# Scores of 64-feature heads with both parts of the queries stacked over 128 rows

## The chip, the cores and the metric

The kernel runs on one core of one Trainium2 chip. The metric is the device time of one launch in microseconds, taken as the median over several runs. TensorE does the matmuls (PE in the profile; its loads of the stationary operand are PEld), VectorE is DVE, ScalarE is ACT, GpSimd is POOL, and SyncE (SP) issues most transfers.

## The reference

Two layers of a decoder trunk over 512 tokens of 1024 features, batch 1, all in float32. Of a layer, what matters here is the attention of mixers A and B, whose heads have 64 features:

```python
# A, for each of 3 head groups of 8 heads; the first group has window 128, dilation 1
logits = jnp.einsum('brnqhd,brnkhd->brnhqk', qb, kb).astype(jnp.float32) * (dh ** -0.5)
bias = bias_table[t5_bucket(step * dilation)].astype(jnp.float32).transpose(2, 0, 1)
logits = jnp.where(valid[None, None, :, None], logits + bias, NEG)
# B: 8 query heads on 2 key heads, window 128, banded blocks
logits = jnp.einsum('bnqhgd,bnchd->bnhgqc', qb, kb).astype(jnp.float32) * (dh ** -0.5)
logits = jnp.where(valid[None, :, None, None], logits + bias, NEG)
# softmax and values follow; C is a latent attention; then gates, output projection, a layer norm,
# a gated feed-forward with a causal convolution (w=3), and a second layer norm
```

With blocks of 128 queries, an undilated A head or a B head looks at its own block of 128 keys and the one before it (the first block at its own alone).

## The kernel before

**Numbers in two parts.** Every matmul operand is kept as a high part, rounded to the type fp32r, and a low part, the rest. `split_to` makes them: ScalarE copies the source into the high part (L177, or L180 with a scale) and VectorE subtracts that from the source (L178, or L181). `mm3` (L171 to L173) adds three products, high by high, low by high and high by low. Weights go the same way: a transfer brings 512 KB, ScalarE and VectorE split it (L76, L77), two pieces ahead of their use.

**Jobs and items.** A job holds the queries and keys of two heads, made by one 128-column projection each (`o1`, 24 matmuls of 512 columns into a bank of the tag `mm`, tiles `qkp`), so that head 0 lies on rows 0 to 63 and head 1 on rows 64 to 127. A layer has 12 A jobs, 4 of them undilated (group g = 0), and 4 B jobs, which share one pair of key heads (`project_bkv`). Each job has four items, one for each block of 128 queries. An item's `scores` makes the scores (tiles `scp`) in PSUM banks of the tag `sc`, of which there are two, and VectorE adds the bias and takes the maximum (L486), ScalarE the exponentials (L489); `turn` transposes them (`ptp`, L500) and splits them (`pT`); `values` multiplies by the values (`op`).

**Three forms of scores.** Dilated A jobs (g > 0) are "joint": the keys are laid out block-diagonally, and one `mm3` over all 128 rows makes both heads' scores in one bank. The others take one bank for each head and three matmuls for each head, ordered so that the two heads alternate; in undilated A and B these use 64 rows (head 0 the upper half, head 1 the lower), in C 96 rows:

```python
pp = [s_bank("scp")[:, :n] for _ in range(2)]
ops = [j.qk(h, slice(t * P, (t + 1) * P), slice(k0, k0 + n)) for h in range(2)]
for a, b, first, last in ((0, 2, True, False), (0, 3, False, False), (1, 2, False, True)):
    for p, o in zip(pp, ops):
        nc.tensor.matmul(p, o[a], o[b], start=first, stop=last)
```

Here n is 256 columns, or 128 for the first block.

**What sets the order.** Projections call `gap`, which starts items as a budget of time allows; a scheduler then places every engine's instructions by readiness and priority, so items of A and B come to stand between the matmuls of the projections and gates that follow, and an item's matmuls may stand apart. Each engine runs its own list in order. Tiles of 1024 columns (queries, keys, values, `pT` and others) come from one pool of 22 slots.

Of the kernel before, what the change touches and what calls it, by code (L numbers as in the profile page):

```python
# [133 lines left out]
def hybrid_trunk(ctx: ExitStack, tc: tile.TileContext, I, out):  # L134
# [20 lines left out]
    def s_bank(name):  # L155
        return bank("sc", 2, name)
# [10 lines left out]
    def slot(name, dtype=F32):  # L167
        return sp.tile([P, 1024], dtype, name=name, tag="s")
# [203 lines left out]
    for l in range(DEPTH):  # L372
# [87 lines left out]
        class Item:  # L460
# [6 lines left out]
            def scores(self):  # L467
                j, t = self.job, self.t
                nk = len(j.keys(t))
                n = nk * P  # L470
                self.sb = tp.tile([P, 512], F32, name="sb", tag="sb", bufs=4) if nk <= 2 else slot("sb")
                self.st = j.stats(t, self)
                v = self.sb[:, :2 * n].rearrange("p (h k) -> p h k", h=2)
                k0 = j.keys(t)[0] * P
                if j.joint:
                    p = s_bank("scp")
                    pp = [p[:, h * n:(h + 1) * n] for h in range(2)]
                    mm3(p[:, :2 * n], *j.qk_joint(slice(t * P, (t + 1) * P), slice(k0, k0 + n)), True, True)
                else:
                    pp = [s_bank("scp")[:, :n] for _ in range(2)]  # L480
                    ops = [j.qk(h, slice(t * P, (t + 1) * P), slice(k0, k0 + n)) for h in range(2)]
# [3 lines that stand above are left out]
                for h in range(2):  # L485
                    nc.vector.tensor_tensor_reduce(v[:, h, :], pp[h], j.bias(h, nk), -j.scale, j.floor(h),  # L486
                                                   ALU.add, ALU.min, self.st[:, h:h + 1])
                for h in range(2):
                    nc.scalar.activation(v[:, h, :], v[:, h, :], AF.Exp, bias=self.st[:, h:h + 1], scale=-1.0,  # L489
                                         accum_out=self.st[:, 2 + h:3 + h])  # L490
# [33 lines left out]
                else:  # L524
                    j.finish(t, self, o)

        def halves(h, q, k, qs, ks):
            b = slice(h * 64, h * 64 + 64)
            return q[b, 0, qs], q[b, 1, qs], k[b, 0, ks], k[b, 1, ks]

        def block_diagonal(src):

# [12 lines left out]
        class JobA:  # L545
# [2 lines left out]

            def __init__(self, hf, g, c, bv, vv):
                self.hf, self.g, self.c, self.bv, self.vv = hf, g, c, bv, vv  # L550
                self.joint = g > 0
                self.vt, self.vh = 2, 2 * c

            def normalize(self, item, n):
# [8 lines left out]
            def stats(self, t, item):  # L563
                item.row = tp.tile([P, 132], F32, name="row", tag="row", bufs=4)
                return item.row[:, P:]

            def qk(self, h, qs, ks):
                return halves(h, self.q, self.k, qs, ks)

            def qk_joint(self, qs, ks):  # L570
                return self.q[:, 0, qs], self.q[:, 1, qs], self.k[0][:, :, ks], self.k[1][:, :, ks]
# [51 lines left out]
        def project_a(l, j):  # L623
# [8 lines left out]
            for c in range(2):  # L632
                job = JobA(hf, g, c, bv, vv)
                for nm in ("q", "k"):
                    w = W.next((l, (j, nm, c)), KT, P)
                    p = mm_bank("qkp")
                    o1(p, w, 0, xT, gap)
                    if g and nm == "k":
                        job.k = block_diagonal(p.rearrange("p (i r) -> p r i", r=4))
                        gap(UNIT / 2)  # L640
                        continue
                    r = slot(nm, F32R).rearrange("p (a n) -> p a n", a=2)
                    setattr(job, nm, r)
                    src, dh, dl = p[:, :], r[:, 0, :], r[:, 1, :]
                    if g:
                        src = src.rearrange("p (i r) -> p r i", r=4)
                        dh, dl = (a.rearrange("p (r i) -> p r i", r=4) for a in (dh, dl))
                    split_to(dh, dl, src, 0.125 if nm == "q" else None)
                    gap(UNIT / 2)
                att.queue.extend(Item(job, t) for t in range(NT))  # L650
            if j % 3 == 2:
# [1 line left out]

        class JobB(JobA):

            g, mixer, joint, direct, vt, vh = 0, 1, False, True, NT, 0

            def __init__(self, i):
                self.i = self.c = i
# [20 lines left out]
            def project(self, l, bv, kv):  # L680
                self.bv, (self.k, self.vv) = bv, kv
                p = mm_bank("qkp")
                o1(p, W.next((l, "bq", self.i), KT, P), 0, xT, gap)
                self.q = slot("q", F32R).rearrange("p (a n) -> p a n", a=2)
                split_to(self.q[:, 0, :], self.q[:, 1, :], p[:, :], 0.125)
                gap(UNIT / 2)

        def scale_rows(item, n):
# [6 lines left out]

        def project_bkv(l):
            w = W.next((l, "bk"), KT, P)
            kk = slot("bk", F32R).rearrange("p (a n) -> p a n", a=2)
            vv = slot("bv", F32R).rearrange("p (t h a d) -> p t h a d", t=4, h=2, a=2)
            p = mm_bank("qkp")  # L700
            o1(p, w, 0, xT, gap)
            split_to(kk[:, 0, :], kk[:, 1, :], p[:, :])
            gap(UNIT / 2)
            p = mm_bank("vp")
            o1(p, W.next((l, "bv"), KT, P), 0, xT, gap)
# [9 lines left out]

        class JobC:

            scale, mixer, joint, direct, vt, vh = C_SCALE, 2, False, True, NT, 0

            def __init__(self, c):  # L720
                self.c = c
# [370 lines left out]
```

## Time and profile before

| | |
|---|---|
| median of 3 runs | 2124.74 us (2123.12 to 2124.78) |
| the profiled execution's own time | 2121.85 us |
| its span, from the first to the last instruction | 2120.0 us |
| PE busy | 2084.7 us, 98% |
| DVE busy | 1198.1 us, 57% |
| ACT busy | 889.9 us, 42% |
| mean TensorE clock granted | 0.998 |

The profile is of one execution. A matmul's row gives its start and its length; successive matmuls overlap in the records, so what one costs the stream is the distance from its start to the next start. Names such as `scp<-k,q` say what is written and, behind the arrow, what is read; a form such as `64*128 64x256` says 64 rows by 128 columns of stationary operand, and 256 columns moved.

### The profile page before, as it was taken

How to read it: one execution, taken by the hardware profiler on the slowest of the kernel's cores; microseconds unless marked ns; L12 is line 12 of the kernel's file. 1: busy time of each engine (PE TensorE's matmuls, PEld its weight loads, DVE VectorE, ACT ScalarE, POOL GpSimd, SP SyncE). 2: the span in 40 equal slices, each digit the busy share in tenths (PEclk: the TensorE clock that was granted, in tenths of full speed). 3: DMA queues.
4: the chain of work that ended last, by engine and by line, in shares of the span. 5: the costliest groups of instructions: out<-in, count | busy, mean ns of one | idle time of the engine just before them, and what ended most of it. 6: DMA issues, size and time to landing. Idle time of an engine off the chain costs nothing. (4 is left out here: it accounts for less than half of the span.)

```text
span 2120.0 us, 29699 instructions
## 1 busy us (share of the span) xinstructions
PE 2084.7 (98%) x11138; PEld 1745.7 (82%) x11138; DVE 1198.1 (57%) x2601; ACT 889.9 (42%) x1906; POOL 185.0 (9%) x333
## 2 busy tenths in 40 slices
PE   8999999999999999999999999999999999999997
PEld 7788887888888888888888888778888888888886
DVE  4455656666546664466464556476565566644655
ACT  4344444655433343244234544455544324423431
POOL 1011211111000100000020212011100010000001
PEclk9999999999999999999999999999999999999999
DMA  6633434223235232332333333342223352323321
GB/s 180 200 85 99 125 94 127 87 74 83 76 118 179 80 100 86 103 100 95 119 110 83 96 118 102 97 122 79 61 78 93 99 181 80 100 90 105 94 95 65
DMA packets 299404, 220.34 MB, mean 104 GB/s; under 512 B 27658, under 2 KB 273371, under 8 KB 298748
## 3 DMA queue, kind: packets, MB, share of 16 engines
q1 hardware_dynamic: 292796, 203.55, 32.8%
q0 software_dynamic: 6464, 14.89, 2.4%
q8 instruction: 88, 1.44, 0.3%
q14 instruction: 56, 0.46, 0.1%
HBM read 201.38 MB, written 22.26 MB: 105 GB/s over the span
## 5 line engine op out<-in xcount | busy, mean ns | idle before, releaser
L77 DVE TENSOR_TENSOR wlo<-wraw,whi 128x1024 fp32r<-128x1024 f32 (+2 forms) x316 | 380.4, 1205 | 417.5 <-ACT whi L76 414.7
L76 ACT ACTIVATE whi<-wraw 128x1024 fp32r<-128x1024 f32 (+2 forms) x316 | 329.2, 1043 | 422.9 <-PE dnp L172 119.7
L172 PE MATMUL up<-xl,whi 128*128 128x512 f32 (+1 forms) x768 | 285.3, 372 | 0.4
L171 PE MATMUL up<-xh,whi 128*128 128x512 f32 (+1 forms) x768 | 284.2, 372 | 0.7 <-ACT xh L324 0.5
L173 PE MATMUL up<-xh,wlo 128*128 128x512 f32 (+1 forms) x768 | 284.5, 371 | 0.0
L171 PE MATMUL qkp<-xh,whi 128*128 128x512 f32 x464 | 185.5, 400 | 0.0
L173 PE MATMUL qkp<-xh,wlo 128*128 128x512 f32 x464 | 185.3, 399 | 0.0
L172 PE MATMUL qkp<-xl,whi 128*128 128x512 f32 x464 | 184.8, 398 | 0.0
L172 PEld LDWEIGHTS up<-xl,whi 128*128 128x128 f32 x768 | 144.6, 188 | 26.0 <-DVE xl L329 1.2
L171 PEld LDWEIGHTS up<-xh,whi 128*128 128x128 f32 x768 | 144.0, 188 | 26.6 <-ACT xh L324 1.6
L173 PEld LDWEIGHTS up<-xh,wlo 128*128 128x128 f32 x768 | 144.5, 188 | 24.9
L171 PE MATMUL gp<-xh,whi 128*128 128x512 f32 x384 | 153.3, 399 | 0.0
L172 PE MATMUL gp<-xl,whi 128*128 128x512 f32 x384 | 152.6, 397 | 0.0
L173 PE MATMUL gp<-xh,wlo 128*128 128x512 f32 x384 | 152.0, 396 | 0.0
L489 ACT ACTIVATE sb<-sb,row 128x128 f32<-128x128 f32 (+1 forms) x192 | 81.0, 423 | 153.6 <-DVE row L486 142.6
L172 PE MATMUL dnp<-wlo,hT 128*128 128x512 f32 x352 | 136.9, 389 | 0.0
L173 PE MATMUL dnp<-whi,hT 128*128 128x512 f32 x352 | 136.8, 389 | 0.0
L171 PE MATMUL dnp<-whi,hT 128*128 128x512 f32 x352 | 135.6, 389 | 0.0
L178 DVE TENSOR_TENSOR pT<-ptp,pT 128x512 fp32r<-128x512 f32 (+1 forms) x176 | 93.8, 540 | 58.8 <-ACT pT L177 58.7
L486 DVE CUSTOM_DVE_ANT_0 sb<-scp,bias 128x128 f32<-128x128 f32 (+1 forms) x192 | 55.7, 321 | 116.4 <-DMA arow<-row 88.5
L177 ACT ACTIVATE pT<-ptp 128x512 fp32r<-128x512 f32 (+1 forms) x176 | 81.6, 474 | 73.0 <-PE ptp L500 71.3
L173 PEld LDWEIGHTS qkp<-xh,wlo 128*128 128x128 f32 x464 | 87.3, 188 | 17.9 <-issue 0.4
(306 smaller groups left out, 4312.7 us busy)
## 6 DMA issues: line engine op xcount, KB each, us to landing
wraw<-in_w_in_dram SPq DMA_DIRECT2D x124, 512.0 KB, 3.8
wraw<-in_w_ffn_up_dram SPq DMA_DIRECT2D x88, 512.0 KB, 3.8
wraw<-in_w_ffn_down_dram SPq DMA_DIRECT2D x40, 512.0 KB, 3.6
wraw<-in_w_branch_dram SPq DMA_DIRECT2D x16, 512.0 KB, 3.4
wraw<-in_w_out_dram SPq DMA_DIRECT2D x16, 512.0 KB, 3.8
arow<-row POOLq DMA_DIRECT2D x96, 66.0 KB, 1.9
ct<-arow SPq DMA_DIRECT2D x16, 396.0 KB, 4.2
od<-o_dram SPq DMA_DIRECT2D x12, 512.0 KB, 4.8
```

The costliest lines, as they stand in the source:

```text
L76: nc.scalar.activation(hi[:, :n], raw[:, :n], AF.Copy)
L77: nc.vector.tensor_tensor(lo[:, :n], raw[:, :n], hi[:, :n].bitcast(F32), ALU.subtract)
L171: nc.tensor.matmul(o, lh, rh, start=start, stop=False)
L172: nc.tensor.matmul(o, lh, rl, start=False, stop=False)
L173: nc.tensor.matmul(o, ll, rh, start=False, stop=stop)
L177: nc.scalar.activation(hi, src, AF.Copy)
L178: nc.vector.tensor_tensor(lo, src, hi.bitcast(F32), ALU.subtract)
L486: nc.vector.tensor_tensor_reduce(v[:, h, :], pp[h], j.bias(h, nk), -j.scale, j.floor(h), ALU.add, ALU.min, self.st[:, h:h + 1])
L489: nc.scalar.activation(v[:, h, :], v[:, h, :], AF.Exp, bias=self.st[:, h:h + 1], scale=-1.0, accum_out=self.st[:, 2 + h:3 + h])
```

## The change

The items of undilated A jobs and of B jobs get a form of their own, `stacked`. For each head, `stack_q` puts the high part of its queries on the head's own 64 rows of a tile and the low part on the other 64 rows. `stack_k` writes the high part of each head's keys to both halves of one tile (`ksh`) and the low part to both halves of a second tile (`ksl`). Two matmuls over 128 rows then make a head's scores, one with `ksh` and one with `ksl`; they also add the product of the two low parts, which was left out before. Both heads lie side by side in one bank of `sc`. For queries ScalarE and VectorE issue two instructions each, on 64 rows, instead of one on 128; for keys, four each instead of one. Keys take two slots instead of one. C and the dilated A jobs stay as they were.

```diff
@@ -476,6 +476,13 @@
                     p = s_bank("scp")
                     pp = [p[:, h * n:(h + 1) * n] for h in range(2)]
                     mm3(p[:, :2 * n], *j.qk_joint(slice(t * P, (t + 1) * P), slice(k0, k0 + n)), True, True)
+                elif j.stacked:
+                    p = s_bank("scp")
+                    pp = [p[:, h * n:(h + 1) * n] for h in range(2)]
+                    for h in range(2):
+                        for i in range(2):
+                            nc.tensor.matmul(pp[h], j.q[:, h, t * P:(t + 1) * P], j.k[i][:, h, k0:k0 + n],
+                                             start=i == 0, stop=i == 1)
                 else:
                     pp = [s_bank("scp")[:, :n] for _ in range(2)]
                     ops = [j.qk(h, slice(t * P, (t + 1) * P), slice(k0, k0 + n)) for h in range(2)]
@@ -524,9 +531,28 @@
                 else:
                     j.finish(t, self, o)
 
-        def halves(h, q, k, qs, ks):
-            b = slice(h * 64, h * 64 + 64)
-            return q[b, 0, qs], q[b, 1, qs], k[b, 0, ks], k[b, 1, ks]
+        HALF = (slice(0, 64), slice(64, 128))
+
+        def stack_q(src):
+
+            r = slot("q", F32R).rearrange("p (h n) -> p h n", h=2)
+            for h in range(2):
+                own, other = HALF[h], HALF[1 - h]
+                nc.scalar.activation(r[own, h, :], src[own], AF.Copy, scale=0.125)
+                nc.vector.scalar_tensor_tensor(r[other, h, :], src[own], 0.125, r[own, h, :].bitcast(F32),
+                                               op0=ALU.mult, op1=ALU.subtract)
+            return r
+
+        def stack_k(src):
+
+            hi, lo = parts = [slot(nm, F32R).rearrange("p (h n) -> p h n", h=2) for nm in ("ksh", "ksl")]
+            for h in range(2):
+                own = HALF[h]
+                for b in (own, HALF[1 - h]):
+                    nc.scalar.activation(hi[b, h, :], src[own], AF.Copy)
+                for b in (own, HALF[1 - h]):
+                    nc.vector.tensor_tensor(lo[b, h, :], src[own], hi[own, h, :].bitcast(F32), ALU.subtract)
+            return parts
 
         def block_diagonal(src):
 
@@ -548,7 +574,7 @@
 
             def __init__(self, hf, g, c, bv, vv):
                 self.hf, self.g, self.c, self.bv, self.vv = hf, g, c, bv, vv
-                self.joint = g > 0
+                self.joint, self.stacked = g > 0, g == 0
                 self.vt, self.vh = 2, 2 * c
 
             def normalize(self, item, n):
@@ -563,9 +589,6 @@
             def stats(self, t, item):
                 item.row = tp.tile([P, 132], F32, name="row", tag="row", bufs=4)
                 return item.row[:, P:]
-
-            def qk(self, h, qs, ks):
-                return halves(h, self.q, self.k, qs, ks)
 
             def qk_joint(self, qs, ks):
                 return self.q[:, 0, qs], self.q[:, 1, qs], self.k[0][:, :, ks], self.k[1][:, :, ks]
@@ -639,13 +662,14 @@
                         job.k = block_diagonal(p.rearrange("p (i r) -> p r i", r=4))
                         gap(UNIT / 2)
                         continue
-                    r = slot(nm, F32R).rearrange("p (a n) -> p a n", a=2)
-                    setattr(job, nm, r)
-                    src, dh, dl = p[:, :], r[:, 0, :], r[:, 1, :]
                     if g:
-                        src = src.rearrange("p (i r) -> p r i", r=4)
-                        dh, dl = (a.rearrange("p (r i) -> p r i", r=4) for a in (dh, dl))
-                    split_to(dh, dl, src, 0.125 if nm == "q" else None)
+                        job.q = r = slot(nm, F32R).rearrange("p (a n) -> p a n", a=2)
+                        dh, dl = (r[:, i, :].rearrange("p (r i) -> p r i", r=4) for i in range(2))
+                        split_to(dh, dl, p.rearrange("p (i r) -> p r i", r=4), 0.125)
+                    elif nm == "q":
+                        job.q = stack_q(p)
+                    else:
+                        job.k = stack_k(p)
                     gap(UNIT / 2)
                 att.queue.extend(Item(job, t) for t in range(NT))
             if j % 3 == 2:
@@ -653,7 +677,7 @@
 
         class JobB(JobA):
 
-            g, mixer, joint, direct, vt, vh = 0, 1, False, True, NT, 0
+            g, mixer, joint, stacked, direct, vt, vh = 0, 1, False, True, True, NT, 0
 
             def __init__(self, i):
                 self.i = self.c = i
@@ -681,8 +705,7 @@
                 self.bv, (self.k, self.vv) = bv, kv
                 p = mm_bank("qkp")
                 o1(p, W.next((l, "bq", self.i), KT, P), 0, xT, gap)
-                self.q = slot("q", F32R).rearrange("p (a n) -> p a n", a=2)
-                split_to(self.q[:, 0, :], self.q[:, 1, :], p[:, :], 0.125)
+                self.q = stack_q(p)
                 gap(UNIT / 2)
 
         def scale_rows(item, n):
@@ -695,11 +718,10 @@
 
         def project_bkv(l):
             w = W.next((l, "bk"), KT, P)
-            kk = slot("bk", F32R).rearrange("p (a n) -> p a n", a=2)
             vv = slot("bv", F32R).rearrange("p (t h a d) -> p t h a d", t=4, h=2, a=2)
             p = mm_bank("qkp")
             o1(p, w, 0, xT, gap)
-            split_to(kk[:, 0, :], kk[:, 1, :], p[:, :])
+            kk = stack_k(p)
             gap(UNIT / 2)
             p = mm_bank("vp")
             o1(p, W.next((l, "bv"), KT, P), 0, xT, gap)
@@ -715,7 +737,7 @@
 
         class JobC:
 
-            scale, mixer, joint, direct, vt, vh = C_SCALE, 2, False, True, NT, 0
+            scale, mixer, joint, stacked, direct, vt, vh = C_SCALE, 2, False, False, True, NT, 0
 
             def __init__(self, c):
                 self.c = c
```

On PE, in the B items of layer 1, the list of before reads as follows at the second and third block of the first B job. `scp_3464` is head 1 of the second block, `scp_3519` head 0 of the third; `bk` are the shared keys, `qkp_3531` the projection of a later job.

```order
L484 MATMUL scp_3464<-bk_3030,q_3289 128x256 x3
L173 MATMUL qkp_3531<-xh_114,wlo_3315 128x512
L171 MATMUL qkp_3531<-xh_114,whi_3314 128x512
L172 MATMUL qkp_3531<-xl_115,whi_3314 128x512
L173 MATMUL qkp_3531<-xh_114,wlo_3315 128x512
L171 MATMUL qkp_3531<-xh_114,whi_3314 128x512
L484 MATMUL scp_3519<-bk_3030,q_3289 128x256 x3
L172 MATMUL qkp_3531<-xl_115,whi_3314 128x512
```

In the changed kernel the third block of the same job (`scp_3514`, both heads) stands so:

```order
L172 MATMUL qkp_3523<-xl_115,whi_3311 128x512
L484 MATMUL scp_3514<-ksh_3085,q_3284 128x256
L484 MATMUL scp_3514<-ksl_3086,q_3284 128x256
L484 MATMUL scp_3514<-ksh_3085,q_3284 128x256
L484 MATMUL scp_3514<-ksl_3086,q_3284 128x256
L173 MATMUL qkp_3523<-xh_114,wlo_3312 128x512
```

Before, the heads of a block stood apart, three matmuls each; now a block's four matmuls stand together between two matmuls of a projection.

On DVE, at the first undilated A job of layer 1, the list of before is this; `wlo` are low parts of weights, `k_644` are the job's keys, `scp_668` and `scp_669` its first block's scores, which VectorE reads.

```order
L77 TENSOR_TENSOR wlo_616<-wraw_431,whi_615 128x1024
L181 SCALAR_TENSOR_TENSOR q_610<-qkp_585,q_610 128x512
L77 TENSOR_TENSOR wlo_650<-wraw_579,whi_649 128x1024
L178 TENSOR_TENSOR k_644<-qkp_619,k_644 128x512
L77 TENSOR_TENSOR wlo_712<-wraw_613,whi_711 128x1024
L181 SCALAR_TENSOR_TENSOR q_692<-qkp_653,q_692 128x512
L486 ISA sb_666,row_667<-scp_668,bias_577 128x128
```

In the changed kernel the same place reads:

```order
L77 TENSOR_TENSOR wlo_618<-wraw_431,whi_617 128x1024
L542 SCALAR_TENSOR_TENSOR q_610<-qkp_585,q_610 64x512 x2
L77 TENSOR_TENSOR wlo_659<-wraw_579,whi_658 128x1024
L554 TENSOR_TENSOR ksl_647<-qkp_621,ksh_646 64x512 x4
L77 TENSOR_TENSOR wlo_717<-wraw_615,whi_716 128x1024
L542 SCALAR_TENSOR_TENSOR q_698<-qkp_662,q_698 64x512 x2
L493 ISA sb_675,row_676<-scp_677,bias_577 128x128
```

The splits stand where they stood, between the same weight pieces; there are two for queries and four for keys in place of one.

## Rows read from the trace of the kernel before

**Rows 1.** The page, part 1: busy time, share of the span, instructions.

```profile
PE 2084.7 (98%) x11138; PEld 1745.7 (82%) x11138; DVE 1198.1 (57%) x2601; ACT 889.9 (42%) x1906; POOL 185.0 (9%) x333
```

**Rows 2.** Waits of PE, whole span: us in total, times, longest us.

```profile
PE xtp L321 <- DMA xin<-in_x_dram: 5.2, 2, 4.8
PE latp L171 <- ACT xh L324: 4.0, 4, 2.9
PE scp L171 <- DVE row L486: 3.5, 4, 1.1
...
PE scp L484 <- DVE bst L486: 2.1, 2, 1.0
```

**Rows 3.** The tile scp: min, median and max ns, first and last start, forms.

```profile
L484 PE MATMUL scp<-k,q x192: 268/278/385, 71.3 to 1383.5; 64*128 64x256 f32 x144, 64*128 64x128 f32 x48
L484 PE MATMUL scp<-bk,q x192: 268/278/386, 340.2 to 1463.6; 64*128 64x256 f32 x144, 64*128 64x128 f32 x48
```

**Rows 4.** Timeline of PE, layer 1, one undilated head: start us, length us, instruction.

```profile
297.51 0.39 PE L172 MATMUL qkp<-xl,whi 128*128 128x512 f32 x1
297.83 0.62 PE L484 MATMUL scp<-k,q 64*128 64x256 f32 x3
298.38 0.50 PE L173 MATMUL qkp<-xh,wlo 128*128 128x512 f32 x1
298.72 0.27 PE L500 MATMUL ptp<-ident,sb 128*128 128x128 f32 x1
```

**Rows 5.** Timeline of PE, layer 2, both heads of an undilated item.

```profile
1123.96 0.39 PE L173 MATMUL vp<-xh,wlo 128*128 128x512 f32 x1
1124.28 0.62 PE L484 MATMUL scp<-k,q 64*128 64x256 f32 x6
1124.83 0.44 PE L500 MATMUL ptp<-ident,sb 128*128 128x128 f32 x2
```

**Rows 6.** Timeline of PE, layer 1, a joint item between projection matmuls.

```profile
184.00 0.39 PE L173 MATMUL qkp<-xh,wlo 128*128 128x512 f32 x1
184.22 0.28 PE L171 MATMUL scp<-kh,q 128*128 128x256 f32 x1
184.34 0.28 PE L172 MATMUL scp<-kl,q 128*128 128x256 f32 x1
184.46 0.28 PE L173 MATMUL scp<-kh,q 128*128 128x256 f32 x1
184.58 0.40 PE L171 MATMUL qkp<-xh,whi 128*128 128x512 f32 x1
```

**Rows 7.** Timeline of PE, layer 1: full-array matmuls of 128 columns.

```profile
341.37 0.27 PE L518 MATMUL op<-vv,pT 128*128 128x128 f32 x1
341.48 0.28 PE L519 MATMUL op<-vv,pT 128*128 128x128 f32 x1
```

**Rows 8.** Windows of the tile scp on PE, the four stretches with 64-row items, summed.

```profile
sum 370.00, PE 59.49; mean PE 14.87
```

**Rows 9.** Timeline of PE: the first and the last of 104 stretches of 64-row matmuls.

```profile
71.25 0.33 PE L484 MATMUL scp<-k,q 64*128 64x128 f32 x2
...
1463.30 0.62 PE L484 MATMUL scp<-bk,q 64*128 64x256 f32 x6
```

**Rows 10.** The tile kh, which is written 64 rows at a time: ACT and DVE rows.

```profile
L177 ACT ACTIVATE kh<-qkp x32: 572/590/596, 110.3 to 1305.3; 64x512 fp32r<-64x512 f32 x32
L178 DVE TENSOR_TENSOR kl<-qkp,kh x32: 671/686/696, 111.9 to 1305.9; 64x512 fp32r<-64x512 f32 x32
```

**Rows 11.** Timelines of ACT and of DVE at the first undilated job's keys.

```profile
66.21 0.58 ACT L177 ACTIVATE k<-qkp 128x512 fp32r<-128x512 f32 x1
...
67.48 0.68 DVE L178 TENSOR_TENSOR k<-qkp,k 128x512 fp32r<-128x512 f32 x1
```

**Rows 12.** Windows, the B items' stretch: length, busy PE, PEld, DVE, ACT, POOL.

```profile
340.00:420.00 80.00, 79.53 (x507) 63.47 (x507) 59.31 (x220) 44.70 (x137) 10.56 (x19) 1.00 0.40 115
```

## The prediction

> **What bounds the kernel now.** I read the page's table of engines first. TensorE is busy for 98% of the span, VectorE for 57%, ScalarE for 42% [rows 1], so the reader is to see one engine that hardly ever stops. Its waits come next: the longest totals are 5.2 us and 4.0 us at the start of the layers, 3.5 us where a joint item waits for VectorE, and 2.1 us in C [rows 2]. A waiting TensorE is therefore worth little here. What counts is how much of the stream its own matmuls take, and that is read from start to start in its timeline.
>
> **What the removed matmuls take.** Undilated A and B issue 192 matmuls each [rows 3]: 64 items (2 layers, 8 jobs, 4 blocks) with two heads and three products. They come in 104 stretches, each between other matmuls; the first and the last are in [rows 9], and more than half of them hold one head alone.
>
> One such stretch, between two projection matmuls, shows three costs [rows 4]. The matmul ahead of it lasts 0.32 us to the next start (297.51 to 297.83). The three of the stretch take 0.55 us (to 298.38). The matmul behind it lasts 0.34 us (to 298.72). A projection matmul of 512 columns elsewhere has 0.22 to 0.23 us, as 184.00 to 184.22 [rows 6]. So entering costs 0.09 us and leaving 0.11 us on top of the stretch.
>
> When both heads stand together, six matmuls also take 0.55 us (1124.28 to 1124.83), with the same 0.32 us ahead [rows 5]. The two heads do run side by side, since six take no longer than three, but a pair then costs 0.18 us.
>
> The joint items beside them use all 128 rows: 0.12 us each for 256 columns (184.22, 184.34, 184.46, 184.58), and nothing at entry or exit [rows 6]. Full-array matmuls of 128 columns follow each other by 0.11 us [rows 7].
>
> The sum over both layers: the recorded time of all 64-row matmuls is 59.5 us [rows 8]. In each stretch the last record runs 0.07 us past the next start (0.62 us against 0.55 us, [rows 4, 5]), so 104 x 0.07 = 7.3 us overlap other work, and 52.2 us remain. From the starts of all 104 stretches I add 10.7 us at entries (about 0.10 us each) and 8.2 us at exits (0.11 us where a projection follows, about 0.05 us where a transpose does). Together 71.1 us.
>
> **What the new matmuls take.** 48 items have 4 x 256 columns and 16 have 4 x 128. By the rates of [rows 6, 7] that is 48 x 0.48 + 16 x 0.44 = 23.0 + 7.0 = 30.1 us, without entry and exit, since every neighbour then uses the full array. The bounds: at 0.11 us for all 256 it would be 28.2 us; if each item met a lag of 0.05 us at its first matmul, 33.3 us. I take 30.1 us, the rate of the same shape. TensorE's stream gets shorter by 71.1 - 30.1 = 41.0 us (38 to 43).
>
> The Trainium skill, "TensorEngine Tiling (Array Packing)", section "Key Properties", says that a change of tiling mode drains TensorE. The 0.09 us and 0.11 us around a stretch agree with it, and by that rule they go entirely, as in the sum. The same page, section "Theoretical Speedup", gives up to twice the speed for a contraction of at most 64, which speaks against stacking; the third rival below takes up that mechanism from rows.
>
> **What the splits add.** Queries: 16 times one more instruction on ScalarE and one on VectorE. Keys: 10 times three more on each. A write of 64 rows by 512 takes 0.59 us on ScalarE and 0.69 us on VectorE [rows 10], no less than 128 rows do (0.58 and 0.68 us, [rows 11]). So 46 x 0.59 = 27 us of ScalarE and 46 x 0.69 = 32 us of VectorE, on engines that are idle for 58% and 43%. Half of the key writes go from one half of the rows to the other, which no row shows; below I bound it by the price above, and above by twice that, and take the price above, as nothing but the destination differs.
>
> Is it on the path? At the first job of a layer the key copy starts at 66.21 us and its subtraction at 67.48 us [rows 11]; the first scores start at 71.25 us [rows 9]. Four copies end at 66.21 + 2.36 = 68.6 us, four subtractions at 67.48 + 2.76 = 70.2 us. That leaves 1 us, and the other jobs stand further from their keys in TensorE's list, by at least one more us of projection matmuls. If the crossing writes cost double, the last ends near 71.6 us, and at worst some tenths are waited for in four of the jobs: under 2 us. The weight splits queued behind are two pieces ahead of their use, and a piece lasts 24 x 0.23 = 5.5 us, so a delay of 2 us is covered. The projection's bank is held 2 us longer, of three that take turns at 5.5 us each; covered too. The extra slot for the keys moves nothing that I find in the lists of the engines.
>
> **New waits.** With 41 us of its own work gone, TensorE meets its helpers sooner. The nearest rows are the joint items' four waits, 0.9 us each [rows 2], and I take four or five such waits, 4 us. One bank for each item in place of two pulls the other way: with two banks, an item can begin while VectorE still reads the one before. Nothing at all to 20 us is possible (second rival).
>
> **The sum.** The profiled execution took 2121.85 us (span 2120.0, and 1.85 around it). 2121.85 - 41.0 + 4 = 2084.9 us. The runs' median lies 2.9 us above this execution, so the forecast is 2088 us, 1.7% less.
>
> **The rivals.**
>
> First, the forecast: TensorE stays the pace, and the 41 us come through less a few. Speaking for it is that the price is read at the place, from start to start. Own range 2079 to 2096 us, 0.74.
>
> Second, VectorE gives back B's half. In B's stretch it is busy for 59.3 of 80.0 us [rows 12], the densest stage. Half of the matmuls are B's [rows 3], so this stage would lose 41.0 / 4 = 10 us in each layer and gain four subtractions, 2.8 us: 62.1 of 70 us, 89%. In that crowd each score waits for a maximum, an exponential and a subtraction in line. If the stage kept its length, 20.5 us would be lost: 2088 - 4 + 20.5 = 2104 us. Against it: 89% is still below full, and ScalarE is at 44.7 us [rows 12]. 0.18.
>
> Third, slower. Pairs of heads run side by side now, and stacking ends that. If the slow pairs and the entry costs came from the items' place and not from the 64-row form, a full-speed pair would cost 0.12 us, three of them 0.36 us, and four stacked matmuls in line 0.48 us: 64 x 0.12 = 7.7 us more at most, 2132 us. For it: six matmuls in the time of three [rows 5]. Against it: the joint items stand in the same company and pay nothing [rows 6], and a single head, with no partner, pays for three. It decides only if a stacked matmul costs over 71.1 / 256 = 0.28 us, more than twice the joint one. 0.04.
>
> Fourth, no change: TensorE's freed time turns into waits, item by item, because the chain of an item's scores, exponentials and transposes sets the pace throughout. 0.64 us lost for each of 64 items would do it, 2125 us. Against it, waits of such items are almost absent now [rows 2]. 0.04.
>
> **How the numbers follow.** The likeliest case gives 2088 us. The range from 2079 us (38 to 43 us gained, no new wait, and a bank freed early) to 2106 us holds the first case and most of the second. About 0.2% is what a measurement of this kernel can tell from no change, 4 us. Faster 0.92 (first two), same 0.04, slower 0.04.
>
> **What would show it.** In the changed profile, four matmuls of 128x256 stand 0.12 us apart, and the one ahead of them has 0.23 us, not 0.32. TensorE's busy time falls by about 40 us. VectorE's rises by some 30 us. Waits of the scores for `ksl`, `ksh` or for VectorE's maxima stay under 1 us each. The forecast is wrong if those waits come in every item of B, if the crossing writes take well over 0.7 us, or if the stacked matmuls follow each other by 0.2 us or more.

## The result, and the profile after

The changed kernel takes 2108.98 us (median of 4 runs, 2104.78 to 2110.94), against 2123.93 us for the kernel before beside it (4 runs, 2121.87 to 2124.78): a ratio of 0.9928, interval 0.9911 to 0.9946. It is 15 us faster where 36 were forecast, and just above the stated range, which ended at 2106 us. Its profiled execution took 2108.23 us, its span is 2106.3 us, 13.7 us less than before, and the mean granted clock is 0.992 where before had 0.998.

The table of engines, part 1 of the page after:

```profile
PE 2054.7 (98%) x11010; PEld 1745.6 (83%) x11010; DVE 1226.4 (58%) x2647; ACT 916.6 (44%) x1952; POOL 185.1 (9%) x333
```

Against [rows 1], TensorE is busy for 30 us less, VectorE for 28 us more and ScalarE for 27 us more. Had TensorE found no new waits, its 30 us would have come off the span; 13.7 did.

Rows of the new tiles, after: shortest, median and longest in ns, first and last start, form.

```profile
L552 ACT ACTIVATE ksh<-qkp x40: 574/594/597, 65.3 to 1350.8; 64x512 fp32r<-64x512 f32 x40
L554 DVE TENSOR_TENSOR ksl<-qkp,ksh x40: 679/688/698, 66.5 to 1353.3; 64x512 fp32r<-64x512 f32 x40
```

The 40 writes of each kind hold the crossing ones, and shortest and longest lie about 20 ns apart: a write into the other half of the rows costs what [rows 10] cost.

The waits of TensorE after, whole span (us in total, times, longest):

```profile
PE op L171 <- ACT ot L529: 7.2, 10, 2.7
PE latp L171 <- ACT xh L324: 4.6, 4, 3.5
PE xtp L321 <- DMA xin<-in_x_dram: 4.6, 1, 4.6
PE scp L171 <- DVE row L493: 3.9, 4, 1.8
PE gp L171 <- ACT gs L899: 3.5, 2, 1.7
PE otp L453 <- issue: 3.3, 2, 2.0
PE scp L484 <- DVE bst L493: 2.7, 2, 1.5
```

Four of these are new against [rows 2]: `op` (the product with the values) for ScalarE's eviction of the item before it, `gp` (a gate) for the activation that empties a gate's bank, `otp` (the transposes of mixer A's finished output), and the stacked scores (L484) for VectorE's maxima; the 2.1 us under the same name in [rows 2] were C's, whose line is now L491. The four lie in one place, the B items' stretch of each layer. Its windows after, layer 1 (stretch, length, busy PE, PEld, DVE, ACT, POOL, granted clock, DMA share, GB/s):

```profile
330.00:340.00 10.00, 10.00 (x62) 8.81 (x60) 8.72 (x35) 7.47 (x24) 1.07 (x2) 1.00 0.61 159
340.00:350.00 10.00, 9.52 (x57) 8.14 (x55) 8.07 (x40) 3.75 (x14) 1.07 (x2) 1.00 0.47 134
350.00:360.00 10.00, 7.25 (x27) 5.81 (x28) 9.71 (x31) 6.03 (x15) 1.08 (x2) 0.83 0.64 188
360.00:370.00 10.00, 9.82 (x66) 8.38 (x65) 9.75 (x34) 7.73 (x19) 1.12 (x2) 1.00 0.24 66
370.00:380.00 10.00, 6.00 (x58) 5.46 (x57) 5.95 (x28) 5.01 (x20) 3.01 (x6) 0.85 0.61 184
380.00:390.00 10.00, 7.75 (x40) 6.37 (x39) 4.04 (x12) 3.62 (x10) 1.18 (x2) 0.67 0.13 34
```

Before, TensorE was busy for 79.53 of the 80 us from 340 on, at a clock of 1.00 [rows 12]. After, three of the windows hold 6.0 to 7.8 us of work, and the clock is granted at 0.67 to 0.85 in them.

How the first of the three begins, in TensorE's timeline after (start, length, instruction, idle time before it and what ended it):

```profile
348.66 0.39 PE L173 MATMUL gp<-xh,wlo 128*128 128x512 f32 x1
348.88 0.28 PE L484 MATMUL scp<-ksh,q 128*128 128x256 f32 x1
349.00 0.28 PE L484 MATMUL scp<-ksl,q 128*128 128x256 f32 x1
349.12 0.28 PE L484 MATMUL scp<-ksh,q 128*128 128x256 f32 x1
349.24 0.28 PE L484 MATMUL scp<-ksl,q 128*128 128x256 f32 x1
351.01 0.39 PE L484 MATMUL scp<-ksh,q 128*128 128x256 f32 x1 [1.50 <-DVE bst L493]
...
353.49 0.80 PE L171 MATMUL gp<-xh,whi 128*128 128x512 f32 x1 [1.74 <-ACT gs L899]
354.09 0.63 PE L172 MATMUL gp<-xl,whi 128*128 128x512 f32 x1
354.51 0.63 PE L173 MATMUL gp<-xh,wlo 128*128 128x512 f32 x1
```

The stacked matmuls are what was forecast: 0.12 us apart, and the gate matmul ahead of them has 0.22 us. Then the next item's scores wait 1.50 us and the next gate 1.74 us, and after these two waits the gate's matmuls stand 0.42 us apart in place of 0.23: the clock's lower level, 1.2 GHz, until 356.2 us.

What VectorE did meanwhile, its timeline after:

```profile
347.25 0.96 DVE L858 TENSOR_TENSOR ct<-ct,cw__3377 128x768 f32<-128x768 f32 x1
...
349.50 0.17 DVE L850 TENSOR_REDUCE cmx<-ct 128x4 f32<-128x12 f32 x1 [0.82 <-DMA ct<-arow]
349.59 0.41 DVE L861 TENSOR_TENSOR ot<-ct 128x256 f32<-128x256 f32 x1
...
350.08 0.46 DVE L493 CUSTOM_DVE_ANT_0 sb<-scp,bias,sink 128x256 f32<-128x256 f32 x1
```

L850 to L862 are `Combine`, which weighs A's three head groups against each other. VectorE's list is kept in order, so the B item's maximum (L493), whose scores began at 348.88 us, ran at 350.08 us, behind a Combine that had waited 0.82 us for its transfer. ScalarE's exponentials stand behind that maximum, and the gate's activation (L899) behind the exponentials:

```profile
350.58 0.51 ACT L496 ACTIVATE sb<-sb,bst 128x256 f32<-128x256 f32 x1 [3.15 <-DVE bst L493]
...
351.69 1.04 ACT L76 ACTIVATE whi<-wraw 128x1024 fp32r<-128x1024 f32 x1
352.75 0.69 ACT L899 ACTIVATE gs<-gp,bg 128x512 f32<-128x512 f32 x1
```

The copy of a weight piece (L76) stands between the two.

The second hole, TensorE's timeline after, from 373 to 388 us:

```profile
377.44 0.37 PE L171 MATMUL op<-pT,bv 128*64 128x128 f32 x1 [2.71 <-ACT ot L529]
...
380.94 0.37 PE L171 MATMUL op<-pT,bv 128*64 128x128 f32 x1 [0.47 <-ACT ot L529]
...
385.36 1.22 PE L453 MATMUL otp<-ident,od 128*128 128x128 f32 x8 [1.31 <-issue]
387.06 0.71 PE L171 MATMUL bp<-oth,whi 128*128 128x512 f32 x1 [0.47 <-ACT oth L177]
```

Here no projection or gate stands between the items: TensorE has only B's items, A's output transposes and their waits. The gate loop explains it: after GATE_LEAD (2) gates it asks for all of A's output (`att.drain`, `load_oT`, whose transposes are `otp`). In the list three gates stand ahead of these transposes, the last of them from 361.70 us, and no further one until 387.57 us.

The first gate of layer 1, first before, then after:

```profile
356.18 0.39 PE L171 MATMUL gp<-xh,whi 128*128 128x512 f32 x1
```

```profile
341.76 0.45 PE L171 MATMUL gp<-xh,whi 128*128 128x512 f32 x1
```

It starts 14.4 us earlier; the output projection starts at 645.9 against 649.2 us, 3.3 us earlier. In layer 2 the first gate is 15.9 us earlier, the end 13.7 us. So the gain arrives up to the gates (by the forecast's prices some 12 us were due there in layer 1), and most of it goes between the gates and the output projection.

The chain behind A's output did not come earlier with the gates. GpSimd issues the write of layer 1's last Combine at almost the same time, first before, then after:

```profile
371.82 0.54 POOL L841 DMA_DIRECT2D o_dram<-ot  x1 [3.56 <-DVE ot L840]
```

```profile
371.59 0.59 POOL L863 DMA_DIRECT2D o_dram<-ot  x1 [0.17 <-issue]
```

### The profile page after: what moved, and what is told of

It reads as the page before. It is cut to its first block, busy times and chain, and to the rows that moved or that the text cites. A ratio compares the mean times of both kernels' runs of the same rounds, so it can differ in the third digit from the quotient of the medians.

```text
span 2106.3 us, 29546 instructions
## 1 busy us (share of the span) xinstructions
PE 2054.7 (98%) x11010; PEld 1745.6 (83%) x11010; DVE 1226.4 (58%) x2647; ACT 916.6 (44%) x1952; POOL 185.1 (9%) x333
## 5 line engine op out<-in xcount | busy, mean ns | idle before, releaser
L76 ACT ACTIVATE whi<-wraw 128x1024 fp32r<-128x1024 f32 (+2 forms) x316 | 328.9, 1043 | 387.6 <-PE dnp L172 117.9
L493 DVE CUSTOM_DVE_ANT_0 sb<-scp,bias 128x128 f32<-128x128 f32 (+1 forms) x192 | 54.2, 321 | 118.9 <-DMA arow<-row 100.6
```

Source lines behind the costliest of these rows:

```text
L76: nc.scalar.activation(hi[:, :n], raw[:, :n], AF.Copy)
```

## The experiments

Edits are to the changed kernel unless said. Times are medians, ratios against the kernel before on the same chip. In ten of the eighteen runs the time fell outside every range that had been stated for it; such a run decides between its theories only where that is said.

**Half the change: A alone, B alone.** In one, B's `stacked` is False and its splits are as before; in the other A's.

```diff
-            g, mixer, joint, stacked, direct, vt, vh = 0, 1, False, True, True, NT, 0
+            g, mixer, joint, stacked, direct, vt, vh = 0, 1, False, False, True, NT, 0
...
-                self.joint, self.stacked = g > 0, g == 0
+                self.joint, self.stacked = g > 0, False
```

> Only undilated A stacked, B as before the change. Theory 1: half of the 41 us is saved and B's stage is braked by its two banks, 2102 to 2107 us. Theory 2: A has most of the key splits (24 of 30 more on each engine), so a loss of two thirds of 28 us is left, 2115 to 2125 us.

> Only B stacked, undilated A as before the change. Theory 1: 20 us saved, and most of the 28 us lost in B's stage is still lost, 2120 to 2132 us. Theory 2: B has few of the splits, so 2105 to 2112 us.

A alone: 2113.47 us, ratio 0.9959 (0.9945 to 0.9974), 9 us. B alone: 2124.88 us, 1.0012 (1.0002 to 1.0021). B's half, half of all stacked matmuls, is worth nothing by itself, and even A's half keeps less than half of its 20 us. The second theory of each blamed the added splits. But B alone has 14 of the 46 added instructions on each engine, A alone 32, and it is B alone that loses its whole 20 us: the loss does not grow with the number of splits.

**A bank for each head**, as before, with stacked matmuls:

```diff
-                    p = s_bank("scp")
-                    pp = [p[:, h * n:(h + 1) * n] for h in range(2)]
+                    pp = [s_bank("scp")[:, :n] for _ in range(2)]
```

> The changed kernel, but each head's stacked scores go to a bank of their own, so an item takes both banks of the tag sc as before the change. Theory 1 (crowding: the matmuls save about 41 us, but with one bank for an item the B items of a layer start too early, VectorE is full for 25 us, and TensorE then waits and loses clock): with the old brake the items spread again, 2085 to 2096 us. Theory 2 (the extra splits on VectorE and ScalarE eat the gain): nothing changes, 2105 to 2112 us.

2104.17 us, 0.9918 (0.9903 to 0.9932): about 2 us better than the changed kernel by the ratios, within their intervals. Where the score banks go is not the main cause; the wait of `op` for ScalarE stays (4.1 us in 3 waits from 300 to 620 us).

**B's items later.** A B item's cost in the budget is doubled, so that `gap` starts fewer of them early.

```diff
+            def cost(self, t):
+                return 2 * (0.4 + 0.3 * len(self.keys(t)))
```

> The changed kernel with the planned cost of a B item doubled, so the gaps give B's items out at half the rate; splits, matmuls and banks as in the changed kernel. Theory 1: VectorE's crowd is spread, 2085 to 2098 us. Theory 2: 2105 to 2112 us.

2129.4 us, 1.0036 (1.0023 to 1.0049): slower than before. The first gate then gains 4.9 us only, and layer 1 ends 7.1 us later than before: what is put off has to be made up after the gates, where less work can lie beside it.

**A longer lead of the gates.** A's output is asked for after four gates, not two. The same constant puts off the points where B's and C's outputs are asked for, and the gates' results lie in the pool of slots.

```diff
-    GATE_LEAD = 2
+    GATE_LEAD = 4
...
-                gs[n] = tp.tile([P, S], F32, name="gs", tag="w2", bufs=4)
+                gs[n] = slot("gs")[:, :S]
```

> The changed kernel with the gates four ahead of the branch matmuls instead of two, their tiles in the pool of slots, so that mixer A's results are asked for two gates (11 us of projection matmuls) later. Theory 1 (chain: TensorE now reaches the point where it needs mixer A's combined result sooner, and the chain that makes it, last A items, transfers, Combine on VectorE, transfers back, does not come sooner, so the saved time returns as waits there): 2085 to 2098 us. Theory 2 (the added splits fill VectorE and ScalarE): 2103 to 2112 us.

2095.47 us, 0.9873 (0.9857 to 0.989): 27 us, almost twice the gain. The same edit to the kernel before is the control:

> The kernel before with the gates four ahead of the branch matmuls, scores unchanged: the control for the longer lead. Theory 1 (the lead pays only because TensorE, sped up by stacking, arrives too early): TensorE hardly waited before, so 2118 to 2126 us. Rival: the lead is a gain of its own, about 13 us as in the changed kernel, 2107 to 2113 us.

2124.52 us, 1.0001 (0.9992 to 1.001). The lead does nothing for the kernel before; the 12 us that it returns were lost by the changed kernel there. With A alone stacked and this lead:

> Only undilated A stacked, with the lead of four. If the saving of the two halves is equal and B's two banks keep VectorE's crowd away, 2100 to 2104 us (20 us saved, nothing lost); if A's half is braked by Combine too, 2108 to 2114 us as without the lead.

2104.01 us, 0.991 (0.9895 to 0.9925): 19 us, all but about 1 us of A's half of the 41. So what a lead of four still loses is in B's half: 27 us less 19 leaves it 8 of its 20. The windows of layer 1 show where, first with the whole change and this lead, then with A alone and this lead:

```profile
350.00:360.00 10.00, 4.86 (x25) 3.89 (x24) 9.29 (x31) 6.18 (x16) 1.62 (x3) 0.70 0.78 223
380.00:390.00 10.00, 10.00 (x64) 8.49 (x64) 7.15 (x30) 6.13 (x21) 1.21 (x2) 1.00 0.54 156
```

```profile
350.00:360.00 10.00, 10.00 (x60) 7.96 (x59) 8.56 (x29) 5.60 (x16) 0.54 (x1) 1.00 0.39 103
```

The lead all but closes the second hole (370 to 390 us; the window 390:400 still holds 8.04 us of work) and not the first, which stands only where B is stacked too, with VectorE busy for 9.29 of 10 us. A lead of six:

> The changed kernel with a lead of six gates. If what a lead of four still loses hangs on the point where mixer A's or B's results are asked for, two more gates bring 4 to 10 us more, 2085 to 2092 us. If it is VectorE's crowd in B's first 30 us, which stands ahead of that point, nothing more, 2093 to 2100 us.

2109.86 us, 0.9936 (0.9921 to 0.9951). In layer 1 the gates' 289th matmul came 28 us earlier than before (24 us with a lead of four), the output projection only 2.4 us (11 us): what a still longer lead gains at the gates is given back behind them. (In the kernel before, a lead of four by itself brings the 289th 12 us forward, since it changes the order.) Why six gates lose what four gain was not tested.

**VectorE's part of Combine.** Three edits: Combine cut to one addition of two groups (the weighting and the third group are left out); its two closing additions on GpSimd; and, as a test of the splits, the crossing halves of the keys copied by GpSimd, so that ScalarE and VectorE have two key instructions each, not four. The last two edits:

```diff
-                nc.vector.tensor_tensor(o2, ct[:, 0, :, :P], ct[:, 1, :, :P], ALU.add)
-                nc.vector.tensor_tensor(o2, o2, ct[:, 2, :, :P], ALU.add)
+                nc.gpsimd.tensor_tensor(o2, ct[:, 0, :, :P], ct[:, 1, :, :P], ALU.add)
+                nc.gpsimd.tensor_tensor(o2, o2, ct[:, 2, :, :P], ALU.add)
```

```diff
-                for b in (own, HALF[1 - h]):
-                    nc.scalar.activation(hi[b, h, :], src[own], AF.Copy)
-                for b in (own, HALF[1 - h]):
-                    nc.vector.tensor_tensor(lo[b, h, :], src[own], hi[own, h, :].bitcast(F32), ALU.subtract)
+                nc.scalar.activation(hi[own, h, :], src[own], AF.Copy)
+                nc.vector.tensor_tensor(lo[own, h, :], src[own], hi[own, h, :].bitcast(F32), ALU.subtract)
+                for z in parts:
+                    nc.gpsimd.tensor_copy(z[HALF[1 - h], h, :], z[own, h, :])
```

> The changed kernel with the Combine of mixer A cut to one addition of two groups (the weighting by the softmax denominators and the third group are left out), some 2.5 us of VectorE work less in each of 16 Combines. Theory 1: that work stands in the chain and in the crowd, 2084 to 2096 us. Theory 2, where only the splits matter: the 40 us of VectorE taken away help as well if they fall in the same crowd, but then the key copies moved to GpSimd must help alike; without crowding, 2103 to 2112 us.

> The changed kernel with the two closing additions of each Combine on GpSimd, 0.8 us of VectorE less in each. Theory 1: VectorE's list is freed a little, but the chain gets longer by GpSimd's slower additions, 2095 to 2110 us. Theory 2: 2103 to 2112 us.

> The changed kernel with the other half of both key tiles copied by GpSimd from the head's own half, so ScalarE and VectorE issue two instructions for keys instead of four each; the rest as changed. Theory 1: no key is split in the stage that loses, 2104 to 2112 us. Theory 2: a third to a half of the lost 28 us comes back, 2092 to 2102 us.

Cut short: 2100.03 us, 0.9893 (0.9878 to 0.9908). Additions on GpSimd: 2107.78 us, 0.9927 (0.9912 to 0.9942), no change. Keys by GpSimd: 2116.31 us, 0.9968 (0.9955 to 0.9981), 8 us worse, though VectorE and ScalarE do less. GpSimd's copies (0.62 us each) stand behind the others and make the keys' chain longer, so this run does not isolate the load of the splits.

**The longer lead and Combine together**, first with the bank for each head, or with the last four Combines queued behind B's items:

```diff
-            if j % 3 == 2:
+            if j == 2:
...
+            if i < 2:
+                att.queue.extend(Combine(1, t) for t in (2 * i, 2 * i + 1))
```

> The changed kernel with the lead of four and a bank for each head. If the early start of B's items, which one bank allows, is a loss beside the chain, the two gains add: 2088 to 2093 us. If the bank only delays what the chain then waits for, the lead hides it: 2094 to 2098 us.

> The changed kernel with the lead of four, and the last four Combines queued behind the first and second B job's items, two each, in place of ahead of all B items. If what is still lost at the start of B's stage is VectorE's list standing behind a Combine that waits for its transfer, 2084 to 2092 us; if it is VectorE's plain load, 2094 to 2100 us.

2101.53 us, 0.9901 (0.9884 to 0.9918), and 2114.66 us, 0.9969 (0.9955 to 0.9983): both worse than the longer lead alone. Then with the cut Combine, and with the additions on GpSimd:

> The changed kernel with the lead of four and Combine cut to one addition (weighting and third group left out). If VectorE's work in B's first 30 us is what is left, 2080 to 2088 us, which would be the whole 41 us. If it is the waits for transfers in front of Combine, whose transfers stay, 2092 to 2098 us.

> The changed kernel with the lead of four and Combine's two closing additions on GpSimd: the same result as the reference, 0.8 us less on VectorE in each Combine. If VectorE's work is what is left, a third of the light Combine's gain, 2088 to 2093 us; otherwise 2094 to 2099 us.

2084.65 us, 0.9819 (0.9804 to 0.9833), and 2088.13 us, 0.9837 (0.9821 to 0.9853). The second computes all that the reference asks for and is faster than both kernels. Its windows in B's stretch:

```profile
340.00:350.00 10.00, 10.00 (x54) 8.52 (x53) 8.38 (x36) 4.22 (x15) 5.21 (x8) 1.00 0.61 188
350.00:360.00 10.00, 8.39 (x47) 6.81 (x46) 9.71 (x26) 7.44 (x20) 2.90 (x3) 1.00 0.48 130
360.00:370.00 10.00, 9.04 (x60) 7.55 (x59) 10.00 (x38) 6.07 (x20) 2.67 (x4) 1.00 0.32 91
370.00:380.00 10.00, 10.00 (x75) 8.80 (x74) 9.02 (x33) 8.00 (x24) 1.75 (x3) 1.00 0.45 132
```

VectorE is as full as in the changed kernel (9.71 and 10.00 of 10 us), yet TensorE's holes are 1 to 1.6 us in place of 2.2 to 4, no wait there is over 1.0 us, and the clock stays at 1.00. A full VectorE alone is thus not what costs the time.

**More of Combine on GpSimd**, its multiplication of all groups (L858) too:

> The stacked kernel with a lead of 4 pieces and Combine's additions on GpSimd (2088 us), and Combine's multiplication of all groups by their weights on GpSimd as well. Theory 1 (what still waits in B's stretch waits for VectorE's share of the work): 2084 to 2087 us, the time of the kernel whose Combine is cut short. Theory 2 (the length of the chain from Combine to the output projection is what is left, and GpSimd is slower at it): 2090 to 2100 us.

2095.18 us, 0.9871 (0.9857 to 0.9886): 7 us of the gain are gone. The multiplication takes 1.5 us on GpSimd and 0.95 us on VectorE, and the window 350:360 of this kernel shows the hole again:

```profile
350.00:360.00 10.00, 5.67 (x29) 5.01 (x28) 9.74 (x24) 6.56 (x16) 4.97 (x7) 0.69 0.45 133
```

So taking load off VectorE helps only while it does not make the chain longer or move items against the gates.

**The controls of the two best**, the kernel before with the same two edits each:

> The kernel before, with the gates' lead of 4 pieces and the two closing additions of Combine on GpSimd; nothing is stacked. Theory 1 (TensorE's own 64-row matmuls set the pace of before, so that a lead and a lighter VectorE free nothing there): within 0.2% of before, 2120 to 2126 us, since the longer lead alone had changed nothing (ratio 1.0001). The gain of the stacked kernel with both edits (2088 us) then belongs to the change. Theory 2 (the lighter Combine is worth its time in either kernel): 8 to 15 us faster, 2109 to 2116 us, and stacking would be worth only some 25 us of the 36.

> The kernel before, with the gates' lead of 4 pieces and Combine cut to one addition of two groups (the weighting and the third group left out): the control of the stacked kernel with the same two edits, which took 2084.65 us. Theory 1 (a lighter VectorE lets the heads of an item stand together, and the price of the 64-row matmuls itself falls with the number of their stretches): TensorE's list has 70 stretches of 64-row matmuls here, against 104 before and 82 with Combine's additions on GpSimd; 12 stretches fewer than that are 6 to 8 us less, 2096 to 2101 us, and stacking is then worth only 11 to 17 us with these edits. Theory 2 (the 64-row matmuls keep their 71 us, and what Combine gives back is a wait): 2118 to 2126 us, and stacking is worth its whole 36 to 41 us.

2105.48 us, 0.9924 (0.9907 to 0.994), and 2105.84 us, 0.9916 (0.9899 to 0.9932). Both gain 16 to 18 us with nothing stacked, outside the stated ranges: more than the first control's second theory allowed, and some 5 us less than the second control's first theory. The theory that these edits free nothing before the change has fallen. As the lead alone gave the kernel before nothing, the gain came with the lighter Combine; a lighter Combine without the lead was not run on it. The windows of L484 over the 64-row items, summed, show where from; first the control with the additions on GpSimd, then the one with the cut Combine:

```profile
sum 708.00, PE 47.47; mean PE 23.74
```

```profile
sum 712.00, PE 42.91; mean PE 21.45
```

The same 384 matmuls took 59.49 us before [rows 8]. In these two kernels TensorE's list holds 82 and 70 stretches of 64-row matmuls in place of 104, 48 and 54 of them with the six matmuls of one whole item, in place of 30. A row shows the form, in TensorE's timeline of the first control:

```profile
370.95 0.61 PE L484 MATMUL scp<-bk,q 64*128 64x256 f32 x6
```

So with a lighter Combine the scheduler places an item's two heads together more often (why was not tested), and then six matmuls share one entry, one exit and 0.55 us [rows 5], where two single heads pay for two [rows 4]. The price does not follow the number of stretches alone: with the lead alone the kernel before has 100 stretches and pays 73 us in the ledger below. The rule of the Trainium skill, "TensorEngine Tiling (Array Packing)", section "Key Properties", that a change of tiling mode drains TensorE, agrees: in these two kernels fewer changes go with less time.

**The ledger.** Worked out from the starts of all matmuls: the price of the undilated A and B scores with their entries and exits; what all the rest of TensorE's stream took beyond the same matmuls at their undisturbed distances (0.227 us for 512 columns, 0.12 for 256, 0.11 for 128), against before; and the span against 2120.0 us.

| kernel | scores | rest, against before | span |
|---|---|---|---|
| before | 70 | | |
| changed | 30 | +27 | -13.7 |
| changed, lead 4 | 30 | +14 | -26.8 |
| changed, lead 4, additions on GpSimd | 30 | +4 | -35.9 |
| changed, lead 4, cut Combine | 30 | +2 | -38.3 |
| A alone | 52 | +10 | -7.8 |
| A alone, lead 4 | 52 | +1 | -17.4 |
| B alone | 51 | +26 | +5.6 |
| before, lead 4 | 73 | -1 | +1.8 |
| before, lead 4, additions on GpSimd | 59 | -6 | -16.9 |
| before, lead 4, cut Combine | 54 | +3 | -12.9 |

The 30 is the forecast's price: inside an item the stacked matmuls stood 0.12 and 0.11 us apart, and what some of them took beyond it (a wait behind them, four at the lower clock with 0.21 us, edges of some hundredths) stands under the rest. The columns add up to the span within 1 us: 30 - 70 + 27 = -13 for the changed kernel. Of its 27, some 17 us are more idle time of TensorE (35.9 against 19.3 us between its first and last matmul), some 9 us are matmuls at the lower clock level, 7 of them in B's stretches, and the remainder is edges.

Two things follow from the ledger. A's half loses 10 us, and the lead brings that to 1. With the lead, the cut Combine brings the rest of the changed kernel from +14 to +2 and leaves that of its control where it was (-1 to +3): what the lead leaves over goes with VectorE's work of Combine, while the control's gain lies in the price of its scores.

## Why the prediction was wrong

**What was right.** The price of the removed matmuls (71 us forecast, 70 by the ledger), that of the new ones (30, at 0.12 and 0.11 us each), the vanished entries and exits, the splits' price of 0.59 and 0.69 us also across the halves, and that the splits at a layer's start hide: the first gate came 14.4 us earlier, and no wait for `ksh` or `ksl` is among TensorE's. Not every neighbour uses the full array, as the forecast had it: B's `op` matmuls use 64 columns, and the first 256-column stacked matmul behind them took 0.17 us in place of 0.12 at 371.35 us; over all items this is within the edges. In the two kernels with the lead of four and a lighter Combine, the scores' 40 us came through but for 2 to 4 us, measured against the kernel before (against their own controls less, as told below).

**The step that failed** is "New waits", taken as 4 us from the joint items' four waits of 0.9 us. It measured 27 us (the ledger), of which the changed kernel's windows in layer 1 show both parts: from 340 to 390 us TensorE was busy for 40.3 of 50 us, and the clock lacked 0.17, 0.15 and 0.33 in three windows of 10 us. For the second part, the clock, the sum had no term at all; it is also why TensorE's busy time fell by 30 us and not by the 40 that were to show. The nearest row was the wrong one: a joint item stands between projections, with other matmuls to fill; B's items stand where the list soon has no others.

**Why there.** The second rival named the place, VectorE and B's crowd, and its 2104 us came nearest; 0.18 was too little for it. It was priced at 20.5 us, as if B's half alone were lost. B alone is indeed worth nothing, but A's half also lost over half of its 20 us (A alone: 9 us). There are two places. One is the second hole: A's output, through Combine, its transfer out and back and `otp`, is asked for after two gates. TensorE reaches the gates 14 us earlier; the last Combine's write is issued only 0.2 us earlier. Moving the point by two gates returned 12 us to the changed kernel and none to the one before, and gave A alone nearly its whole half: for these 12 of the 27 us the cause is shown. The other is the first hole: B's stacked items meet VectorE's list with the Combines in it. There the lead gives nothing, and the cut Combine takes a further 12 us off the ledger's rest, none off its control's. That with this lead a further 7 us came by taking 32 additions of 0.42 us off VectorE is measured; which of two it was, the free place in VectorE's line or the scheduler's other order of items, stays open, since each such edit also lays out the lists anew.

**What was not thought of.** The 71 us were read as the price of the 64-row form, but they were the price of this layout of it: stacking takes 40 us off it, and letting the heads stand together more often takes off 11 to 16 us. So the two gains overlap. Against their own controls the stacked scores are worth 27 us (lead 4), 18 us (lead 4, additions on GpSimd, 0.9837 against 0.9924 of about 2123 us) and 21 us (cut Combine, 0.9819 against 0.9916).

**The other rivals.** Slower did not come: the condition, 0.28 us for each stacked matmul, was far off. No change by waits in each item did not come either: the waits are few and long (ten for `op`, two for `gp`), not 64 of 0.64 us.

## What to carry to other kernels

A gain on the busiest engine is worth what the next meeting point of the list lets through: look up what the engine waits for there, and by how much that comes earlier, before the gain is summed. The nearest wait in a trace is a bound only if its place has as much other work to fill in as the place in question. And give each supporting edit its control on the old kernel: here the lead with a lighter Combine was worth 16 to 18 us without the change.

## What was not expected of the hardware

After waits of 1.50 and 1.74 us, close together, in a stream that is otherwise busy for 98%, the matmuls ran at 1.2 GHz for 2.7 us (353.5 to 356.2 us, 0.42 us each in place of 0.23). In the window 380:390 the granted clock is 0.67. By the distances, the lower level cost some 6 us in layer 1's stretch, on top of the waits, but only some 1.6 us in layer 2's: there the second hole (7.0 and 8.5 us of work in two windows of 10, from 1415 us) left the clock at 1.00. Two additions that take 0.42 us each on VectorE take 0.75 and 0.96 us on GpSimd, and yet are better there with a lead of four gates (7 us, and 16 us in the kernel before with this lead), while they make no difference in the changed kernel with a lead of two.
